# One hand-set line for the gates, the first conv tiles and w_out's sums: a hybrid attention and mLSTM encoder layer on one core

## The chip, the core and the metric

The kernel runs on one core of one Trainium2 chip. The metric is the device time of one execution in microseconds (us); the number given for a kernel is the median over its runs. All data and results are f32. Engines carry the short names of the profile: PE multiplies matrices (PEld is its loading of weights), DVE, ACT and POOL work on vectors, and SP does nothing here but issue DMAs, in the order in which they stand on it. What SP issues for a value that isn't ready yet makes all later DMAs wait.

## The reference, cut to what matters

```python
hmix = rms_norm(x, g_norm1) * (1.0 + scale1) + shift1
q_a, k_a, v_a, q_m, k_m, v_m, o_m, gates = jnp.split(hmix @ w_in, IN_SPLITS, axis=-1)
att = rms_norm(banded_attention(q_a, k_a, v_a, sink), g_attn_out)
qk = silu(centred_dwconv(concat([q_m, k_m]), conv_w, conv_b))        # width 3
i_f, f_f, i_b, f_b = jnp.split(gates + b_gates, 4, axis=-1)
h_m = rms_norm(mlstm(q_m, k_m, v_m, i_f, f_f) + flip(mlstm(flip(...), i_b, f_b)), g_mlstm_out)
h_m = sigmoid(o_m) * h_m
x = x + gate1 * (jnp.concatenate([att, h_m], axis=-1) @ w_out)
gte, up = jnp.split((rms_norm(x, g_norm2) * (1.0 + scale2) + shift2) @ w_ffn_in, 2, axis=-1)
return rms_norm(x + gate2 * ((silu(gte) * up) @ w_ffn_out), g_final)
```

There are 2048 positions of 1024 features, 8 attention heads of 64 and 4 mLSTM heads of 128, and a feed-forward width of 2816. The mLSTM gates pass through a log-sigmoid and running sums and maxima over chunks of 128 positions before any mLSTM product can use them.

## The kernel before

**Stages.** First come norm 1 and the projections with positions on the partitions (v, gates), then the projections with features on the partitions, the four mLSTM heads, the attention, the output projection in eight pairs of 128-position blocks (p0 to p7), norm 2, and the feed-forward network. The two large products, `out_proj` and the network, are formed by Strassen-like schemes with seven products in place of eight: `w_out` is loaded, multiplied by the gate and added up into seven operands, which go to DRAM as `wo_d` (`w_out_ops`); the mixed rows are added up into seven operands by `Pair.s1`, `s4`, `both`, `sums`.

**The fill queue.** PE's instructions stand in an order written out by hand. `fill` holds generators of work that waits for little; `pull(n)` issues the next `n` matmuls of it between the steps of the stage that runs. The projections are such work: `conv_tile(j, h)` makes one 128-feature tile of q or k of head `h` in four blocks of 24 matmuls (`proj_mm` into the PSUM tile `gps`). After each block ACT copies it to `cacc` and its ends to `edge`; DVE adds the two neighbours (L444, L445, and L447, L448 for the seams to the previous block), and `finish` applies silu to the block before (ACT `ctanh`, DVE L435) and stores it to `qk_d`. The order on the other engines is set by a scheduler.

**Gates chain.** After the projections of norm 1 a chain of small steps turns the 16 gate columns (`gn`) into the scan results: PE transposes, ACT and DVE steps on 128x128 tiles (named `gates` in listings), four DVE scans, then the chunk ends go to DRAM and come back as one row (`st_d`, then `sr`), eight short DVE scans over it (`mn`), and the results go out and back again (`rw_d`, then `gates` and `dec`); at the end rows go to `bc_d` and three tiles are transposed (`gates_end`). Beside it PE runs 165 matmuls of `fill`, then the end of the two conv tiles of head 0 and 60 more, and then `mlstm(0)` begins.

**mLSTM heads.** Each head loads `mqk` (q and k) and `mv`, does a backward pass (`kn`, `ktp`, `kvp`: keys times values, state `cb`) and then a forward pass with scores (`sps`, times a decay `sc`) and products (`num`, `den`). POOL prepares `ng` (L592) and `qs` (L597) for the scores. At half of the fill steps of heads 0 and 1, one step of `w_out_ops` is put beside: per unit of 128 columns of each half two products on POOL (L832, 128x256), four differences (L836, 128x128), and stores from `bx`, `by`, `ts`; 16 units in all. `proj_cols` loads each tile's weights and splits them (`whi` on ACT, `wlo` on POOL L234).

**First pair and out_proj.** `Pair` holds the mixed rows of a pair: `square` (L938) forms the squares and their sums `msq` on ACT and POOL, `columns` turns them by a matmul with ones into `aps` on PE, `rsqrt` (L101 to L108) and `diagonal` follow on DVE, PE spreads it as `arb`, `scale` multiplies. For the first pair `first_pair` does this during the attention; `both` (L982) makes two operands `mA`, `mS`. `start_wo(u)` and `finish_wo(u)` load operand `u` of w_out and split it (ACT L911, DVE L912). Inside pair p, step i of the loop sets when the next pair's squares, columns and rsqrt come, and `Rows.step(i)` does norm 2's sums of the pair before: its blocks `n` are turned, added (POOL L1200) and stored to `hop_d` (`put`, L1163). `oslots` and `mring` are rings of free tiles.

Of the kernel before, what the change touches and what calls it, by code (L numbers as in the profile page):

```python
# [36 lines left out]
def hybrid_layer_kernel(  # L37
# [184 lines left out]
    def load_w(src, shape, gate=None):  # L222

        pl, i = wslots[0]
        wslots.rotate(-1)
        r = pl.tile([P, D], F32, tag="wraw", name="wraw", bufs=1)
        hi = pl.tile([P, D], F32R, tag=f"w{i}h", name="whi", bufs=1)
        lo = pl.tile([P, D], F32R, tag=f"w{i}l", name="wlo", bufs=1)
        v = lambda t: t.rearrange("p (a b) -> p a b", a=shape[0])
        sp.dma_start(v(r), src)  # L230
        if gate is not None:
            pool.tensor_tensor(v(r), v(r), gate, MUL)
        act.activation(hi, r, AF.Copy)
        pool.tensor_tensor(lo, r, hi.bitcast(F32), SUB)  # L234
        return v(hi), v(lo)

    def proj_cols(c0):
        return load_w(w_in[:, c0:c0 + P].rearrange("(k p) c -> p k c", p=P), (KT, P))
# [5 lines left out]
    with tc.tile_pool(name="sw", bufs=2, side="right", reuse_waits="tile") as sw:  # L244
# [114 lines left out]
        gn = cp.tile([P, 2, 2, HM, NT], F32, tag="gn", name="gn", bufs=1)  # L359
# [64 lines left out]
    def conv_tile(j, h, w=None):  # L424

        w = w or proj_cols((C_QM, C_KM)[j] + h * P)
# [5 lines left out]
        def finish(a, n):  # L432
            t = s2.tile([P, 512], F32, tag="ctanh", name="ctanh")
            act.activation(t, a, AF.Tanh)  # L434
            dve.scalar_tensor_tensor(a, t, 1.0, a, ADD, MUL)  # L435
            sp.dma_start(qk_d[j, h, n], a)

        for n in range(NB):
            ps = bank("g", "gps")
            yield from proj_mm(ps, w, n)  # L440
# [5 lines left out]
            if prev is not None:  # L446
                dve.scalar_tensor_tensor(a[:, 0:1], edge[:, 2 * n - 1:2 * n], w0, a[:, 0:1], MUL, ADD)  # L447
                dve.scalar_tensor_tensor(prev[:, 511:512], edge[:, 2 * n:2 * n + 1], w2, prev[:, 511:512], MUL, ADD)  # L448
                finish(prev, n - 1)
            prev = a  # L450
        finish(prev, NB - 1)
# [279 lines left out]
    ps = bank("c", "gps")  # L731
    gnf = gn.rearrange("p y d h c -> p y (d h c)")
    for y in range(2):
        pe.transpose(ps[:, y * P:(y + 1) * P], gnf[:, y, :], ident)

    t2 = s2.tile([P, 512], F32, tag="cacc", name="gt2", bufs=3)[:, :P]
    dve.memset(s2.tile([P, 512], F32, tag="ctanh", name="gt3")[:, 0:1], 0.0)
# [7 lines left out]
    ig, fg = gt("ig"), gt("fg")  # L745
    act.activation(ig, ps[:, :P], AF.Copy)
    act.activation(fg, ps[:, P:2 * P], AF.Copy)
    e, u, l = gt("ge"), gt("gu"), gt("gl")
    dve.scalar_tensor_tensor(e, fg, -1.0, fg, MUL, MIN)
    act.activation(e, e, AF.Exp)  # L750
    dve.tensor_scalar(u, e, 1.0, None, ADD)
    act.activation(l, u, AF.Ln)
    dve.scalar_tensor_tensor(t2, u, -1.0, e, ADD, SUB)
    dve.reciprocal(u, u)
    dve.tensor_tensor(t2, t2, u, MUL)
    dve.tensor_tensor(l, t2, l, SUB)
    dve.scalar_tensor_tensor(l, fg, 0.0, l, MIN, ADD)
    b, cm, zr = gt("gb"), gt("gcm"), gt("gz")
    r = cp.tile([P, 2, P], F32, tag="gn", name="grr", bufs=1)[:, 0, :]
    dve.memset(zr, 0.0)  # L760
    lo_, hi_ = slice(0, 64), slice(64, 128)
    dve.tensor_tensor_scan(b[lo_], ones[lo_], l[lo_], 0.0, MUL, ADD)
    dve.tensor_tensor_scan(b[hi_, ::-1], ones[hi_, ::-1], l[hi_, ::-1], 0.0, MUL, ADD)
    dve.tensor_tensor(r, ig, b, SUB)
    dve.tensor_tensor_scan(cm[lo_], zr[lo_], r[lo_], -3e38, ADD, MAX)
    dve.tensor_tensor_scan(cm[hi_, ::-1], zr[hi_, ::-1], r[hi_, ::-1], -3e38, ADD, MAX)
    st = gt("gst", 2)
    for sl, j in ((lo_, 127), (hi_, 0)):
        dve.tensor_copy(st[sl, 0:1], b[sl, j:j + 1])
        dve.tensor_tensor(st[sl, 1:2], b[sl, j:j + 1], cm[sl, j:j + 1], ADD)  # L770
    sp.dma_start(st_d.rearrange("j r -> r j"), st)
    sr = s2.tile([1, 2, P], F32, name="sr", bufs=1)
    sp.dma_start(sr, st_d.rearrange("(o j) r -> o j r", o=1))
    mn = s2.tile([1, P], F32, name="mn", bufs=1)
    rw = s2.tile([1, 3, P], F32, name="rw", bufs=1)
    dve.memset(rw, 0.0)
    for d in range(2):
        for h in range(HM):
            q = slice(d * 64 + h * NT, d * 64 + (h + 1) * NT)
            o_, b_, a_ = mn[:, q], sr[:, 0, q], sr[:, 1, q]  # L780
            if d:
                o_, b_, a_ = o_[:, ::-1], b_[:, ::-1], a_[:, ::-1]
            dve.tensor_tensor_scan(o_, b_, a_, 0.0, ADD, MAX)
    mpv = rw[:, 0, :].rearrange("o (q c) -> o q c", c=NT)
    mnv = mn.rearrange("o (q c) -> o q c", c=NT)
    dve.tensor_copy(mpv[:, 0:4, 1:], mnv[:, 0:4, :-1])
    dve.tensor_copy(mpv[:, 4:8, :-1], mnv[:, 4:8, 1:])
    dve.tensor_tensor(rw[:, 1, :], sr[:, 0, :], mn, SUB)
    dve.tensor_tensor(rw[:, 2, :], rw[:, 1, :], rw[:, 0, :], ADD)
    act.activation(rw[:, 2, :], rw[:, 2, :], AF.Exp)  # L790
    sp.dma_start(rw_d.rearrange("(o j) r -> o j r", o=1), rw)
    mc = gt("gmc", 2)
    sp.dma_start(mc, rw_d[0:2].rearrange("j r -> r j"))
    sp.dma_start(dec, rw_d[2].partition_broadcast(P))
    ux, it, em, wr = gt("gux"), gt("git"), gt("gem"), gt("gwr")
    dve.tensor_scalar(ux, cm, mc[:, 0:1], None, MAX)
    act.activation(it, ux, AF.Exp, bias=mc[:, 0:1], scale=-1.0)
    dve.tensor_scalar(it, it, float(128 ** -0.5), None, MUL)
    dve.tensor_tensor(em, b, ux, ADD)
    act.activation(em, em, AF.Exp, scale=-1.0)  # L800
    act.activation(wr, r, AF.Exp, bias=mc[:, 1:2])
    dve.tensor_scalar(ux, ux, -1.0, None, MUL)
    for d, sl in ((0, lo_), (1, hi_)):
        sp.dma_start(bc_d[:, :, d, :].rearrange("h c t -> (h c) t"), ux[sl])
        sp.dma_start(bc_d[:, :, 2 + d, :].rearrange("h c t -> (h c) t"), it[sl])
    def gates_end():
# [299 lines left out]
    for u in (2, 3):  # L1106
        start_wo(u)
# [657 lines left out]
```

## Time and profile before

| | |
|---|---|
| runs before (us) | 2411.76, 2414.21, 2411.64; median 2411.76 |
| profiled execution | 2408.62 us, span 2406.8 us |
| granted PE clock, mean | 0.976 |
| busy share of the span | PE 95%, PEld 79%, DVE 66%, ACT 44%, POOL 43% |
| DMA | 393.47 MB, mean 163 GB/s |

The profile is one execution. From its span's start, norm 1 and the first projections take until 194 us, the gates chain with the first conv tiles until 258.1, the heads end at 367.2, 475.4, 564.4 and 654.5, the attention at 867, and the first pair of `out_proj` begins at 898. The network runs to the end. Lines (L420 and so on) are those of the kernel before; in listings of the changed kernel the numbers are its own.

### The profile page before, as it was taken

How to read it: one execution, taken by the hardware profiler on the slowest of the kernel's cores; microseconds unless marked ns; L12 is line 12 of the kernel's file. 1: busy time of each engine (PE TensorE's matmuls, PEld its weight loads, DVE VectorE, ACT ScalarE, POOL GpSimd, SP SyncE). 2: the span in 40 equal slices, each digit the busy share in tenths (PEclk: the TensorE clock that was granted, in tenths of full speed). 3: DMA queues.
4: the chain of work that ended last, by engine and by line, in shares of the span. 5: the costliest groups of instructions: out<-in, count | busy, mean ns of one | idle time of the engine just before them, and what ended most of it. 6: DMA issues, size and time to landing. Idle time of an engine off the chain costs nothing.

```text
span 2406.8 us, 32761 instructions
## 1 busy us (share of the span) xinstructions
PE 2275.5 (95%) x10801; PEld 1889.9 (79%) x10801; DVE 1587.8 (66%) x3078; ACT 1062.4 (44%) x2157; POOL 1032.1 (43%) x922
## 2 busy tenths in 40 slices
PE   5998888899899998998999999999999999999998
PEld 4987777788788877777887878788888888888886
DVE  6775575775688858768655776755565536684584
ACT  4523444454377755526444444534433323223352
POOL 1001564343333424434655565555656536493020
PEclk9999999999999999999999999999999999999999
DMA  7574666577675565665343452533333264452452
GB/s 290 175 243 110 180 187 185 151 207 218 172 200 175 172 216 188 228 227 189 123 158 101 153 175 92 210 97 114 101 106 109 88 212 151 136 174 96 135 201 94
DMA packets 370881, 393.47 MB, mean 163 GB/s; under 512 B 24862, under 2 KB 268568, under 8 KB 370712
## 3 DMA queue, kind: packets, MB, share of 16 engines
q1 hardware_dynamic: 370712, 391.39, 51.4%
q8 instruction: 85, 1.39, 0.2%
q14 instruction: 84, 0.69, 0.1%
HBM read 272.12 MB, written 119.19 MB: 163 GB/s over the span
## 4 chain that ended last, share of the span: by engine, by line
PE 72%; DVE 8%; DMA 8%; issue 4%; POOL 3%; ACT 3%; SPq 1%; POOLq 0%; ACTq 0%; DVEq 0%
PE fp L56 11%; PE fp L57 11%; PE fp L58 11%; PE gps L420 8%; PE fo L58 6%; PE fo L56 6%; PE fo L57 5%; PE ops L56 2%; PE ops L57 2%; PE ops L58 2%; DMA bc<-bc_d 1%; PE atp L709 1%; DMA vst_d<-vs 1%; DVE macc L336 1%; PE as L686 1%
## 5 line engine op out<-in xcount | busy, mean ns | idle before, releaser
L420 PE MATMUL gps<-hT,whi 128*128 128x512 f32 x1088 | 403.3, 426 | 4.6 <-ACT ctanh L434 4.6
L56 PE MATMUL fo<-w,ah 128*128 128x512 f32 x616 | 242.3, 393 | 2.5 <-ACT ah L1549 2.5
L58 PE MATMUL fo<-w,al 128*128 128x512 f32 x616 | 242.5, 394 | 0.3 <-DVE al L1550 0.3
L57 PE MATMUL fo<-w,ah 128*128 128x512 f32 x616 | 242.0, 393 | 0.0
L420 PE MATMUL gps<-hT,wlo 128*128 128x512 f32 x544 | 231.6, 426 | 0.0
L420 PEld LDWEIGHTS gps<-hT,whi 128*128 128x128 f32 x1088 | 205.8, 195 | 30.8 <-ACT ctanh L434 5.0
L56 PE MATMUL fp<-T,S 128*128 128x512 f32 x528 | 211.5, 401 | 13.1 <-ACT u L1460 6.7
L57 PE MATMUL fp<-T,S 128*128 128x512 f32 x528 | 209.7, 397 | 0.0
L58 PE MATMUL fp<-T,S 128*128 128x512 f32 x528 | 209.7, 397 | 0.0
L1550 DVE TENSOR_TENSOR al<-al,ah 128x1024 fp32r<-128x1024 f32 x77 | 114.4, 1490 | 126.2 <-ACT ah L1549 126.1
L1307 DVE TENSOR_TENSOR A<-graw,A 128x512 fp32r<-128x512 f32 x86 | 106.2, 1254 | 116.5 <-ACT A L1306 116.5
L1549 ACT ACTIVATE ah<-al 128x1024 fp32r<-128x1024 f32 x77 | 81.5, 1060 | 193.9 <-DMA al<-a_d 191.0
L56 PEld LDWEIGHTS fo<-w,ah 128*128 128x128 f32 x616 | 115.9, 188 | 29.2 <-ACT ah L1549 3.0
L58 PE MATMUL fp<-B,A 128*128 128x512 f32 x352 | 137.6, 391 | 0.0
L56 PE MATMUL fp<-B,A 128*128 128x512 f32 x352 | 137.6, 391 | 0.0
L57 PE MATMUL fp<-B,A 128*128 128x512 f32 x352 | 137.6, 391 | 0.0
L58 PEld LDWEIGHTS fo<-w,al 128*128 128x128 f32 x616 | 115.7, 188 | 27.8 <-DVE al L1550 1.5
L57 PEld LDWEIGHTS fo<-w,ah 128*128 128x128 f32 x616 | 115.9, 188 | 26.4
L56 PEld LDWEIGHTS fp<-T,S 128*128 128x128 f32 x528 | 101.1, 191 | 37.3 <-ACT u L1460 8.2
L702 POOL TENSOR_SCALAR ap<-ap,adn 128x384 f32<-128x384 f32 (+1 forms) x128 | 72.9, 588 | 130.9 <-DVE adn L700 57.2
L1307 DVE TENSOR_TENSOR S<-sf,S 128x512 fp32r<-128x512 f32 x86 | 88.9, 1036 | 47.3 <-ACT S L1306 47.2
L58 PEld LDWEIGHTS fp<-T,S 128*128 128x128 f32 x528 | 101.0, 191 | 22.8
(411 smaller groups left out, 6125.0 us busy)
## 6 DMA issues: line engine op xcount, KB each, us to landing
al<-a_d SPq DMA_DIRECT2D x77, 512.0 KB
wmod<-in_w_mod_dram SPq DMA_DIRECT2D x48, 512.0 KB
graw<-in_w_ffn_in_dram SPq DMA_DIRECT2D x43, 512.0 KB
a_d<-ka SPq DMA_DIRECT2D x66, 256.0 KB
bc<-bc_d SPq DMA_DIRECT2D x64, 256.0 KB
hop_d<-n SPq DMA_DIRECT2D x56, 256.0 KB
a_d<-u SPq DMA_DIRECT2D x55, 256.0 KB
mqk<-qk_d SPq DMA_DIRECT2D x48, 256.0 KB
```

The source lines that it names most:

```text
L56: pe.matmul(o, lh, rh, start=first, stop=False, skip_group_check=skip)
L57: pe.matmul(o, lh, rl, start=False, stop=False, skip_group_check=skip)
L58: pe.matmul(o, ll, rh, start=False, stop=last, skip_group_check=skip)
L336: dve.scalar_tensor_tensor(acc, w[:, i, :], sc_col[:, k + i:k + i + 1], acc, MUL, ADD)
L420: pe.matmul(ps, w[i == 2][:, k, :], hT[n](i == 1, k), start=(k == 0 and i == 0), stop=(k == KT - 1 and i == 2))
L686: pe.matmul(s[:, :NK], self.q[:, g, :], self.kk[:, 0, :NK], start=True, stop=False)
L702: pool.tensor_scalar(self.p[g][:, :self.NK], self.p[g][:, :self.NK], dn[:, g:g + 1], 0.0, MUL, ADD)
L709: pe.transpose(tp[:, g * P:(g + 1) * P], self.p[g][:, i * P:(i + 1) * P], ident)
L1307: dve.tensor_tensor(t[:, 1, :], f, t[:, 0, :].bitcast(F32), SUB)
L1549: act.activation(ah, al.bitcast(F32), AF.Copy)
L1550: dve.tensor_tensor(al, al.bitcast(F32), ah.bitcast(F32), SUB)
```

## The change

It rewrites the order around the gates chain and moves w_out's sums into it.

- `gates()` and `w_out_ops()` become generators that yield the number of the next matmul of `fill` at which to go on. A loop over 252 matmuls (two conv tiles and 60 more) steps both by these numbers, and in it DVE, ACT, POOL and SP keep the order of the code as PE does already.
- w_out's units are twice as wide: 8 units instead of 16, each with two products of 128x512 and four differences of 128x256, all in that stretch; the heads have none. Tiles for them are taken from the rings of tiles that the heads use later (`mqk` with 4, `bc` with 3, `og`, `hst`).
- In the first two conv tiles `finish` of a block is put at matmuls 6 and 14 of the next block. The weights of the third tile are loaded at matmul 100 and split at 130, the last block of head 0 (`load_last`) comes at 192, and the chain's final transposes at 140.
- `first_pair` keeps only loads, squares and their sums, beside the attention; its columns, rsqrt, diagonal, scale and `sums` come between the attention and p0, where six of the seven `both` (before: four) and `finish_wo` 1 to 4 (before: 1 to 3) now stand too. In p0 there remain `finish_wo` at steps 5 and 12 (before: 0, 6 and 12) and `both` at step 8 (before: 2, 5 and 8).
- In all pairs `columns` moves from step 7 to 9, rsqrt from 8 to 10, the previous pair's scale from 12 to 13, and the sums of norm 2 by about one step; loads of the second kind come at 8 instead of 10. The second T3 of a pair is put in the tile `oth`, no longer in the ring of nine tiles from which `new` takes.
- Three rings take the weight tiles `w1` ahead of `w0`.

```diff
-    pull(165)
-    gates_end()
+    steps = [gates(), w_out_ops()]
+    due = [0, next(steps[1])]
     hand.enter_context(tc.manual_schedule(engines={mybir.EngineType.PE}))
+    win.enter_context(tc.manual_schedule(engines={getattr(mybir.EngineType, e) for e in ("DVE", "Activation", "Pool", "SP")}))
...
+    for i in range(2 * 96 + 60):
+        for j, g in enumerate(steps):
+            while due[j] <= i:
+                due[j] = next(g)
+        if i == 100:
+            w3 = cols_steps(C_KM + P)
+            next(w3)
...
+        elif i == 192:
+            last = load_last(0)
+        pull(1)
+    win.close()
...
     for h in range(HM):
-        i = 0
-        while any(f is g for f in fill for g in convs[h]):
-            pull(1)
-            i += 1
-            if i % 2 == 0:
-                next(wops, None)
-        last = load_last(h)
-        for i in range(60):
-            pull(1)
-            if i % 2 == 0:
-                next(wops, None)
+        if h:
+            for g in convs[h]:
+                finish_fill(g)
+            last = load_last(h)
+            pull(60)
         mlstm(h, 3, 8, last)
...
+                bx, by = ready
+                pool.tensor_tensor(bx, bx, gb, MUL)
+                yield at + 6
+                pool.tensor_tensor(by, by, gb, MUL)
+                yield at + 8
+                for o in out_:
+                    sp.dma_start(*o)
+                ta = s2.tile([P, 2, 256], F32, tag="bc", name="ts", bufs=3)
+                tb = s2.tile([P, 2, 256], F32, tag="hst", name="ts")
+                for t, f, g in ((ta[:, 1], bx[:, 1], bx[:, 0]), (tb[:, 0], by[:, 1], bx[:, 1]),
+                                (ta[:, 0], by[:, 1], ta[:, 1]), (tb[:, 1], by[:, 0], ta[:, 0])):
+                    pool.tensor_tensor(t, f, g, SUB)
+                    yield at + 12
+                yield at + 18
+                if (c_, k) != (1, 3):
+                    ready = w_out_load(*((c_, k + 1) if k < 3 else (1, 0)))
...
+                at += 26
...
+        yield 44
+        sp.dma_start(st_d.rearrange("j r -> r j"), st)
...
+        yield 64
...
+            dve.tensor_tensor_scan(o_, b_, a_, 0.0, ADD, MAX)
...
+        yield 81
+        sp.dma_start(rw_d.rearrange("(o j) r -> o j r", o=1), rw)
...
+            for i, _ in enumerate(proj_mm(ps, w, n)):
+                if end and i in (6, 14):
+                    next(end, None)
+                yield True
...
-                if i in (0, 6, 12):
-                    finish_wo(4 + i // 6)
-                if i in (2, 5, 8):
+                if i in (5, 12):
+                    finish_wo(4 + (i + 2) // 7)
+                if i == 8:
                     cur.both()
...
-                if i == 7:
+                if i == 9:
                     ps = bank("a", "aps")
...
+                t3 = wp.tile([P, 512], F32, tag="oth", name="n3", bufs=1) if g else self.new()
```

SP's rows in the gates chain before, from the store of the gate row to the second return of the chain; `mv` is head 0's first load of values:

```order
L411 DMA gate_d<-mod 128x8x1
L407 DMA vaug_d<-va 128x516
L510 DMA mv<-vaug_d 128x4x129 x2
L771 DMA st_d<-gates 128x2x1
L773 DMA sr<-st_d 1x256
L436 DMA qk_d<-cacc 128x512
L791 DMA rw_d<-rw 1x384
L436 DMA qk_d<-cacc 128x512
L793 DMA gates<-rw_d 128x2x1
L794 DMA dec<-rw_d 128x128
```

SP's rows there in the changed kernel; the loads and the six stores of w_out's first unit and the loads of its second stand directly ahead of the first row:

```order
L787 DMA st_d<-gates 128x2x1
L789 DMA sr<-st_d 1x256
L844 DMA bx<-in_w_out_dram 128x2x256
L844 DMA by<-in_w_out_dram 128x2x256
L870 DMA wo_d<-bx 128x256
L870 DMA wo_d<-by 128x256 x2
L870 DMA wo_d<-ts 128x256 x2
L870 DMA wo_d<-ts 128x2x256
L438 DMA qk_d<-cacc 128x512
L844 DMA bx<-in_w_out_dram 128x2x256
L844 DMA by<-in_w_out_dram 128x2x256
L810 DMA rw_d<-rw 1x384
```

The chain's stores now stand between w_out's loads and stores, and `mv` comes only after w_out's seventh unit.

POOL's rows in head 0 before, a little after its first scores are prepared:

```order
L234 TENSOR_TENSOR wlo<-wraw,whi 128x1024
L832 TENSOR_TENSOR bx<-bx,gb 128x256
L836 TENSOR_TENSOR ts<-bx 128x128
L597 TENSOR_TENSOR qs<-mqk,bc 128x256 x2
L832 TENSOR_TENSOR by<-by,gb 128x256
L836 TENSOR_TENSOR ts<-by,bx 128x128
L836 TENSOR_TENSOR ts<-by,ts 128x128 x2
L592 TENSOR_TENSOR ng<-bc,maskb 128x256 x2
L597 TENSOR_TENSOR qs<-mqk,bc 128x256
```

POOL's rows in the changed kernel from w_out's last unit into head 0:

```order
L865 TENSOR_TENSOR bx<-bx,gb 128x512
L867 TENSOR_TENSOR by<-by,gb 128x512
L875 TENSOR_TENSOR ts<-bx 128x256
L875 TENSOR_TENSOR ts<-by,bx 128x256
L875 TENSOR_TENSOR ts<-by,ts 128x256 x2
L233 TENSOR_TENSOR wlo<-wraw,whi 128x1024
L601 TENSOR_TENSOR ng<-bc,maskb 128x256
L606 TENSOR_TENSOR qs<-mqk,bc 128x256
L601 TENSOR_TENSOR ng<-bc,maskb 128x256
L606 TENSOR_TENSOR qs<-mqk,bc 128x256
```

No work of w_out stands among `ng` and `qs` any more; all of it stands ahead of the first `ng`.

DVE's rows before at the beginning of p0 (L958 and L955 scale the second pair, `xr` takes a finished product of p0):

```order
L912 TENSOR_TENSOR wo<-wo 128x1024 x4
L958 SCALAR_TENSOR_TENSOR mm<-og,mm 128x1024
L955 SCALAR_TENSOR_TENSOR ma<-ma,cols,arb 128x2x128 x4
L982 TENSOR_TENSOR mS_10626<-ma,mS_10626 128x512
L1090 TENSOR_TENSOR xr<-xr,ops 128x512
L982 TENSOR_TENSOR mS_10644<-mm,mS_10644 128x512
L912 TENSOR_TENSOR wo<-wo 128x1024 x2
```

DVE's rows there in the changed kernel:

```order
L968 TENSOR_TENSOR wo<-wo 128x1024 x2
L1038 TENSOR_TENSOR mS_10472<-ma,mS_10472 128x512
L1038 TENSOR_TENSOR mS_10475<-mm,mS_10475 128x512
L1014 SCALAR_TENSOR_TENSOR mm<-og,mm 128x1024
L1011 SCALAR_TENSOR_TENSOR ma<-ma,cols,arb 128x2x128 x4
L1142 TENSOR_TENSOR xr<-xr,ops 128x512
L968 TENSOR_TENSOR wo<-wo 128x1024 x2
```

Two of the four `wo` rows now stand ahead of the last operands of the first pair, and no operand stands between the scale of the second pair and the first `xr`.

More of the change, by code (lines that the diff above doesn't have):

```diff
@@ L448, in conv_tile @@
                 dve.scalar_tensor_tensor(prev[:, 511:512], edge[:, 2 * n:2 * n + 1], w2, prev[:, 511:512], MUL, ADD)
-                finish(prev, n - 1)
+                end = finish(prev, n - 1)
+                if not ws_:
+                    deque(end, 0)
             prev = a
-        finish(prev, NB - 1)
+        for f in (end, finish(prev, NB - 1)):
+            deque(f, 0)
     def qk_att(pl, tags, j):
@@ L766, in hybrid_layer_kernel @@
[L766 to L785, printed above, removed]
@@ L843, in hybrid_layer_kernel, with w_out_load, w_out_gate @@
-    wops = w_out_ops()
-    hand = ExitStack()
+        yield 1 << 30
+    def w_out_load(c_, k):
+        r = [s2.tile([P, 2, 256], F32, tag="mqk", name=t, bufs=4) for t in ("bx", "by")]
+        for t, k_ in zip(r, (k, k + 4)):
+            sp.dma_start(t, w_out[k_ * P:(k_ + 1) * P].rearrange("p (m c) -> p m c", m=2)[:, :, c_ * 256:(c_ + 1) * 256])
+        return r
+    def w_out_gate(c_):
+        gb = (wp.tile([P, 2, 256], F32, tag="oth", name="gb", bufs=1) if c_ else
+              s2.tile([P, 2, 256], F32, tag="og", name="gb", bufs=1))
+        for m in range(2):
+            sp.dma_start(gb[:, m, :], gate_d[0, m * 512 + c_ * 256:m * 512 + (c_ + 1) * 256].partition_broadcast(P))
+        return gb
@@ L873, in hybrid_layer_kernel @@
         finish_fill(g)
-    assert not fill and not later and next(wops, None) is None
-    wqs.close()
+    assert not fill and not later
     s2s.close()
@@ L1104, in hybrid_layer_kernel @@
     xr = [load_xr(nxt.tt)]
+    ps = bank("a", "aps")
+    for i in range(2):
+        pe.matmul(ps[:, i:i + 1], nxt.t[:, 2 + i], ones[:, 0:1], start=True, stop=True)
+    nxt.diagonal(rsqrt(w0, ps[:, :2], 2, 512, "ar", 1), nxt.t[:, 0:2])
     finish_fill(lasts[1])
@@ L1107, in hybrid_layer_kernel @@
         start_wo(u)
+    pull(10)
+    nxt.scale()
+    finish_wo(1)
+    nxt.sums(nxt.t.rearrange("p k t -> p (k t)"))
     nxt.both()
@@ L1116, in hybrid_layer_kernel @@
         nx2.square(i, sq[:, i])
-    pull(16)
+    finish_wo(2)
+    finish_fill(lasts[2])
+    for u in (4, 5):
+        start_wo(u)
     ps = bank("a", "aps")
@@ L1134, in hybrid_layer_kernel @@
     start_wo(6)
+    for _ in range(2):
+        nxt.both()
     OPS = ("B11", "B21", "T2", "T1", "T3", "B22", "T4")
```

257 lines of the change are left out of this document (139 added, 118 removed).

## The prediction, made blind

> **What bounds the kernel.** I read the page's first and fourth parts, then a table of stages, then the list of waits stage by stage.
>
> ```profile
> span 2406.8 us, 32761 instructions
> ...
> PE 2275.5 (95%) x10801; PEld 1889.9 (79%) x10801; DVE 1587.8 (66%) x3078; ACT 1062.4 (44%) x2157; POOL 1032.1 (43%) x922
> ...
> PE 72%; DVE 8%; DMA 8%; issue 4%; POOL 3%; ACT 3%; SPq 1%; POOLq 0%; ACTq 0%; DVEq 0%
> ```
>
> PE is busy 95% of the span and carries 72% of the chain that ended last. So the time that can be won without taking matmuls away is PE's idle time, and the extra length of matmuls after idle time. The table of stages says where both lie. Its columns are the stretch, its length, busy us (and instructions) of PE, PEld, DVE, ACT and POOL, PE's granted clock, DMA share and GB/s.
>
> ```profile
> 194.00:258.10 64.10, 59.54 (x260) 48.79 (x258) 33.00 (x79) 22.77 (x49) 14.86 (x19) 0.97 0.44 119
> 258.10:367.20 109.10, 90.65 (x475) 76.11 (x474) 69.66 (x233) 46.18 (x144) 62.20 (x93) 0.91 0.65 186
> 367.20:475.40 108.20, 90.85 (x482) 75.76 (x481) 72.01 (x234) 46.68 (x146) 49.39 (x67) 0.92 0.58 171
> 475.40:564.40 89.00, 85.61 (x488) 72.94 (x486) 59.48 (x213) 42.22 (x132) 32.05 (x38) 0.98 0.71 203
> 654.50:867.00 212.50, 205.29 (x1137) 175.00 (x1138) 171.73 (x500) 161.50 (x431) 84.86 (x137) 1.00 0.63 186
> 867.00:900.00 33.00, 31.48 (x140) 25.73 (x139) 13.35 (x25) 11.27 (x17) 7.09 (x6) 0.97 0.79 257
> 900.00:930.00 30.00, 22.47 (x84) 17.50 (x83) 27.62 (x44) 15.39 (x24) 9.72 (x8) 0.83 0.40 128
> ```
>
> Rows two to four are mLSTM heads 0, 1 and 2. They issue nearly the same number of matmuls (475, 482, 488), but heads 0 and 1 take 109.1 and 108.2 us and head 2 takes 89.0. POOL is busy 62.2 and 49.4 us in the first two and 32.1 in the third, which has nothing of w_out. The last row, the start of p0, has PE idle for 7.5 of 30 us and DVE busy for 27.6.
>
> **Part 1: the heads lose w_out.** PE's waits in heads 0 and 1, and then in head 2 (engine, line waited at, who ended the wait, us in total, times, longest):
>
> ```profile
> PE sps L599 <- DVE sc L601: 12.1, 6, 3.7
> PE ktp L538 <- ACT og L648: 5.1, 1, 5.1
> PE kvp L548 <- DVE den L629: 5.0, 1, 5.0
> PE sps L599 <- DMA mqk<-qk_d: 4.8, 1, 4.8
> ```
>
> ```profile
> PE kvp L548 <- DVE den L629: 1.8, 1, 1.8
> PE sps L599 <- DVE sc L601: 0.9, 1, 0.9
> ```
>
> POOL's and SP's own waits between 150 and 600 us say what made these late:
>
> ```profile
> POOL bx L832 <- DMA bx<-in_w_out_dram: 47.7, 13, 11.3
> ```
>
> ```profile
> SPq L529 <- POOL qs L597: 47.3, 28, 4.6
> SPq L839 <- POOL bx L832: 30.4, 12, 4.1
> ```
>
> POOL stood 47.7 us before w_out's `bx`, and `ng`, which the scores need, is queued behind it in the order listings. SP stood 30.4 us before stores of `bx`, and `mqk`, `mv` and `bc` loads are queued behind these. Without w_out both queues hold only the head's own work, as in head 2. If heads 0 and 1 came down to head 2's time, that would be 20.1 + 19.2 = 39.3 us. But they keep something that head 2 has less of: conv tiles, whose sums and silu run on DVE. DVE is busy 69.7 and 72.0 us there against 59.5, 23 us more for both heads; I put a third of it, 8 us, on the path, since the scores wait for DVE in head 2 as well. That makes 39 less 8: **-31 us**, from -24 (half of the waits that look like w_out's remain somewhere) to -38. No cover is needed for this: the POOL work of w_out is moved ahead, and its DMAs as well.
>
> **Part 2: the gates window gains w_out.** What the chain's returns cost now, from SP's rows (start, length, line), DVE's first scan over the returned row, and PE:
>
> ```profile
> 204.63 1.32 SPq L510 DMA_DIRECT2D mv<-vaug_d  x2
> 206.05 0.45 SPq L771 DMA_DIRECT2D st_d<-gates  x1
> 214.17 0.25 SPq L773 DMA_DIRECT2D sr<-st_d  x1
> ```
>
> ```profile
> 216.95 0.78 DVE L783 TENSOR_TENSOR_SCAN mn<-sr 1x16 f32<-1x16 f32 x8 [7.31 <-DMA sr<-st_d]
> ```
>
> ```profile
> 220.57 1.19 PE L420 MATMUL gps<-hT,whi 128*128 128x512 f32 x2 [4.56 <-ACT ctanh L434]
> ```
>
> The chain's store goes out at 206.05, SP stands for it until 214.17, the row is back at 216.95, and only then does DVE get to the third conv block, so PE waits 4.56 us for a free `gps`. The stretch has no other wait of that size. In the changed order the third block's sums still stand behind those scans, so the wait stays and moves with the chain. What makes the chain later: the first block's two sums now come ahead of the chain's second half; `st_d` stands behind six stores of w_out's first unit, and `rw_d` behind the second unit's stores and the fourth unit's loads. The stores also share DMA queues with the gate and value stores, which were landed by 204.63, when `mv` could go. That gives `st_d` at about 209 to 214, 3 to 8 us later.
>
> POOL's own price is worked out from the same operations at other sizes (mean ns behind the bar):
>
> ```profile
> L597 POOL TENSOR_TENSOR qs<-mqk,bc 128x256 f32<-128x256 f32 x64 | 47.6, 746 | 27.2 <-DMA mqk<-qk_d 16.6 <-PE num L622 6.8 <-issue 2.7
> ...
> L639 POOL TENSOR_TENSOR hst<-hst,mry 128x512 f32<-128x512 f32 x16 | 16.6, 1040 | 36.3 <-DVE mry L108 26.7 <-ACT mjk L636 3.7 <-DVE den L629 2.7
> ```
>
> ```profile
> 261.96 0.56 SPq L828 DMA_DIRECT2D bx<-in_w_out_dram  x1
> ```
>
> ```profile
> 265.26 0.90 POOL L832 TENSOR_TENSOR bx<-bx,gb 128x256 f32<-128x256 f32 x1 [4.79 <-DMA bx<-in_w_out_dram]
> ```
>
> A unit is two products of 128x512 (1.04 us, or 1.5 if doubled from 128x256) and four differences of 128x256: 2 x 1.04 + 4 x 0.746 = 5.1 us, with the other price 6.0. Eight units are 41 to 48 us of a window of 64, and a load takes 265.26 - 261.96 = 3.3 us. Loads of a unit need the tiles of the unit two before, so its stores must have landed. While SP stands at `sr`, until about 219, POOL can have only the first two units; six are left, and at 7 to 8 us each (5.1 to 6.0, and what is not hidden of store and load) they end at 261 to 267, when the window, delayed itself, ends at 262 to 266. Their last stores stand on SP ahead of most of head 0's `mqk` and `mv`, so head 0 may begin a few us late. I add up: the chain 3 to 8 us later, matmuls at a lower clock behind a longer wait (1 to 2), and 0 to 6 us for the loads of head 0: **+10 us**, the upper middle of 4 to 16. The low end is -6, if the wait of 4.56 us and its slow matmuls go, since `finish` is now set between the matmuls of the next block. The high end is +20, the rival below.
>
> The final transposes now stand at matmul 140. A matmul takes 59.54 / 260 = 0.229 us, so PE is there at 194 + 32 = 226 plus its wait, at 232 to 238, and the chain's second return and its exponentials must be through by then, within some 12 us of the scans. If they are late by a few us, PE waits that long; this is inside the 4 to 16. The third tile's weights at matmuls 100 and 130 are an existing load and split at another place: 0, hidden by the first two tiles' matmuls.
>
> **Part 3: the first pair.** Waits of PE inside the attention, then from 867 to 930, and then of p4 and p5 (1000 to 1040):
>
> ```profile
> PE aps L989 <- DVE aptl L127: 1.7, 2, 1.0
> ...
> PE arb L953 <- DVE aptl L127: 1.3, 1, 1.3
> ```
>
> ```profile
> PE aps L989 <- POOL msq L942: 4.9, 4, 2.7
> PE ops L56 <- DVE xr L1090: 4.2, 2, 3.5
> ```
>
> ```profile
> PE aps L989 <- POOL msq L942: 5.9, 4, 2.2
> ```
>
> ```profile
> 997.83 1.29 POOL L1200 TENSOR_TENSOR n<-n,n 128x512 f32<-128x512 f32 x1 [3.03 <-DMA hop_d<-n]
> ```
>
> In the attention the columns and the spread of the first pair's norm wait behind attention work on DVE, 3.0 us; those instructions are moved behind it: **-3.0**, from -3 to 0. What remains there, squares and POOL sums, lies beside PE's 205 of 212 us.
>
> At p0's start PE idles 7.5 us, most of it for `msq` and for `xr`. DVE's order puts four `wo` rows and the scale of the second pair ahead of the first `xr`; in the changed order two `wo` rows, two operands and the scale of the second pair. What is taken out of p0 lands in the stretch before (867 to 900), where DVE is busy 13.4 of 33 us and so has 20 us of room, and PE has the last tiles of the fill queue to do. The first pair's own new chain (columns, rsqrt of 12 small DVE steps, spread, scale) is covered by the 10 matmuls and by start_wo, which may not last. The squares' waits move from step 7 to 9, two steps later, of three matmuls each: 6 x 0.229 = 1.4 us, by which such waits get shorter. Of 7.5 us of idling and about 3 us of slower matmuls (clock 0.83) I take **-6**, from -10 to -2.
>
> In p4 and p5 the waits for `msq` stem from `n`: POOL waited 3.03 us for a store to land because the ring of nine was full. The second T3 in `oth` takes one use of the ring away, and columns stand later: **-5** of 5.9 and of the slow matmuls behind them, from -9 to -3. The remaining pairs show no such wait, so the shift by a step costs nothing there.
>
> Ring orders (`w1` ahead of `w0`): 0, from -1 to 1. The feed-forward network is the same code.
>
> **The sum.** -31 + 10 - 3 - 6 - 5 = -35 us against the profiled execution of 2408.6, thus 2373.6. The median of the runs shown is 3.1 us above it, so I forecast **2377 us**.
>
> **Rivals.** *B, POOL and DVE block each other in the window.* The row of a one-column DVE step with two operands in SBUF (ns least, median, most), and two conv steps in head 0, where POOL is busy 57% of the time:
>
> ```profile
> L448 DVE SCALAR_TENSOR_TENSOR cacc<-edge,cvw,cacc x24: 208/212/1743, 206.7 to 496.5; 128x1 f32<-128x1 f32 x24
> ```
>
> ```profile
> L435 DVE SCALAR_TENSOR_TENSOR cacc<-ctanh,cacc 128x512 f32<-128x512 f32 x10 | 7.8, 776 | 1.8 <-ACT ctanh L434 1.6
> L445 DVE SCALAR_TENSOR_TENSOR cacc<-gps,cvw,cacc 128x511 f32<-128x511 f32 x10 | 7.4, 740 | 0.0
> ```
>
> A step of 0.21 us sometimes takes 1.74: it is held for up to 1.5 us. L445, which reads one operand from PSUM, isn't lengthened. In the window POOL would be busy most of the time with steps of 0.75 to 1.0 us, and the chain has about 20 steps of two SBUF operands. At half a POOL step each (0.5) that is 10 us more on the chain, and three such steps in each of the window's ten conv blocks are 15 us more on DVE, which is busy 33.0 of the 64.1 us and can still take them. Then part 2 is +20 to +25 and the time 2387 to 2392; I take 2390. The Trainium skill, page "SBUF — State Buffer", section "Who interferes with whom", states that a DVE instruction with two SBUF inputs contends with a GpSimd instruction that reads SBUF, and that the loser fully blocks. By that rule, the trace agrees: 1743 ns against 212, and 740 for the step with a PSUM operand. It speaks against putting the sums beside the chain.
>
> *C, the window is smooth:* `st_d` is as early as now, the 4.56 us go, and POOL ends in time. -31 - 5 - 3 - 6 - 5 = -50, and 2362. Against it stand SP's six stores ahead of `st_d`.
>
> *D, the heads stay slow:* PE's waits for DVE `sc` (12.1 us) would be due to DVE at 65%, and conv work, not to POOL. Then part 1 gives -8 and the time is 2400. Against it: POOL's 47.7 us of waiting before `bx`, with `ng` behind.
>
> *E, the other side:* the units are paced by their round trip through SP's one line, load 3.3, POOL 5 to 6, store 3 to 5, since a load stands behind stores that wait for POOL, and head 0's loads stand behind the last unit. The gains without part 2 are 45 us; head 0 would have to begin at 258 + 45 = 303. With two units done by 219 and some 4 us of loads at the end, that is (303 - 219 - 4) / 6 = 13.3 us per unit: from there on the kernel is slower, at 14.5 us per unit by 7 us: 2419. For it speaks that SP stood 30.4 us before stores of `bx`; against it that two units have tiles at a time.
>
> **How the numbers follow.** Chances: the forecast 0.45, B 0.2, C 0.15, D 0.1, E 0.1. The likeliest case gives 2377 with its own range of 2366 to 2386. The range of 2356 to 2402 takes in C, B and D and leaves out E, and what is worse than their ends. A measurement of this kernel can tell about 0.2% (4.8 us) from no change. The forecast, B, C and most of D are faster: 0.86; same (2407 to 2416.6), an end of D and the threshold of E: 0.05; slower: 0.09.
>
> **What the changed profile would show.** Right: heads 0 and 1 at 90 to 95 us each with no POOL wait for `bx` in them; the window ending at 262 to 270, one PE wait of 5 to 12 us for `ctanh` in it, `st_d` at 209 to 214; no `aps` or `arb` wait in the attention; p0's start with less than 4 us of PE idling. Wrong: `sps` waits of over 8 us for DVE in heads 0 and 1 with POOL free (D); a first `ktp` of head 0 that waits over 10 us for `mqk` (E, or B if DVE's small steps in the window take over 0.7 us each); new `aps` waits at 880 to 900, where the first pair's chain has little cover, which would eat part 3.

## The result, and the profile after

The changed kernel took 2396.32 us (median of 9 runs, 2391.49 to 2403.93) against 2411.64 us (9 runs): ratio 0.9941, interval 0.9924 to 0.9957. That is 15.3 us less, where 35 were forecast. Its profiled execution took 2403.93 us, the longest of the nine, so single stages of it are read together with those of the experiments that share their code.

First come rows of the view of one tile of PE, of the kernel before and then of the changed one. Behind the count stand ns (least, median, most) and the time of the first and the last; the first times cut the span into stages.

```profile
L538 PE MATMUL ktp<-ident,mqk x64: 270/272/476, 258.1 to 580.9; 128*128 128x128 f32 x64
L686 PE MATMUL as<-ak,aq x128: 276/333/420, 654.7 to 856.9; 128*128 128x384 f32 x112, 128*128 128x256 f32 x16
L56 PE MATMUL ops<-wo,mS x128: 387/393/792, 909.5 to 1086.0; 128*128 128x512 f32 x128
L56 PE MATMUL fp<-T,S x528: 389/389/795, 1094.8 to 1962.3; 128*128 128x512 f32 x176
```

```profile
L547 PE MATMUL ktp<-ident,mqk x64: 270/271/329, 277.5 to 570.7; 128*128 128x128 f32 x64
L695 PE MATMUL as<-ak,aq x128: 276/335/550, 645.7 to 847.9; 128*128 128x384 f32 x112, 128*128 128x256 f32 x16
L56 PE MATMUL ops<-wo,mS x128: 387/393/792, 899.5 to 1078.8; 128*128 128x512 f32 x128
L56 PE MATMUL fp<-T,S x528: 389/389/794, 1087.7 to 1954.5; 128*128 128x512 f32 x176
```

| stage | before | after | forecast change | change |
|---|---|---|---|---|
| window: last store of values (194.6, 196.5) to head 0's `ktp` | 63.5 | 81.0 | +10 | +17.5 |
| heads: to the first `as` | 396.6 | 368.2 | -31 | -28.4 |
| attention and p0's beginning: to the first `ops` | 254.8 | 253.8 | -9 | -1.0 |
| `out_proj`: to the first `fp` | 185.3 | 188.2 | -5 | +2.9 |
| network: to the end of the span | 1312.0 | 1314.4 | 0 | +2.4 |

The heads in the table of stages (the second and third row are heads 0 and 1, without POOL's waits for `bx`), ahead of them the window:

```profile
194.00:277.50 83.50, 63.63 (x268) 51.36 (x266) 38.34 (x75) 19.04 (x40) 48.37 (x49) 0.89 0.64 185
277.50:371.10 93.60, 84.21 (x473) 70.97 (x472) 69.34 (x236) 48.87 (x151) 36.38 (x41) 0.98 0.60 181
371.10:464.10 93.00, 84.56 (x482) 70.30 (x481) 70.81 (x234) 47.15 (x147) 34.58 (x39) 1.00 0.53 159
```

Heads 0 and 1 fell from 109.1 and 108.2 us to 93.6 and 93.0, and DVE is as busy in them as before. The window holds POOL's 48 us, and PE idles 20 of its 83 us there. Where PE's wait comes from is read backwards through four engines: PE, DVE, SP, POOL (the number in brackets is the idle time before the row):

```profile
232.91 1.19 PE L420 MATMUL gps<-hT,whi 128*128 128x512 f32 x2 [14.99 <-DVE cacc L451]
```

```profile
228.85 0.78 DVE L800 TENSOR_TENSOR_SCAN mn<-sr 1x16 f32<-1x16 f32 x8 [13.16 <-DMA sr<-st_d]
```

```profile
213.67 2.56 SPq L870 DMA_DIRECT2D wo_d<-ts  x3
216.33 0.41 SPq L787 DMA_DIRECT2D st_d<-gates  x1
226.21 0.25 SPq L789 DMA_DIRECT2D sr<-st_d  x1
```

```profile
209.71 1.29 POOL L865 TENSOR_TENSOR bx<-bx,gb 128x512 f32<-128x512 f32 x1 [22.39 <-DMA gb<-gate_d]
```

PE waits 15 us for a free `gps`, since the third conv block's sums stand on DVE behind the scans over `sr`. `st_d` went out only at 216.33, behind the first unit's stores, though its data were ready at 208.8. Those stores waited for POOL, whose first product waited until 209.71 for `gb`. PE's waits at p0's start, and then in the other pairs:

```profile
PE ops L56 <- DVE xr L1142: 5.2, 1, 5.2
PE aps L1045 <- POOL msq L998: 5.0, 2, 4.3
```

```profile
PE ops L56 <- DVE xr L1142: 9.1, 7, 2.5
```

The waits for `msq` in p4 and p5 are gone, and seven waits for `xr` stand in their place. At p0's start PE waits 5.0 us for `msq` and 5.2 for `xr`, no less than before (4.9 and 4.2). PE's rows for `xr` there, two of the kernel before and one of the changed:

```profile
909.54 0.79 PE L56 MATMUL ops<-wo,mS 128*128 128x512 f32 x1 [0.66 <-DVE xr L1090]
920.45 0.77 PE L56 MATMUL ops<-wo,mS 128*128 128x512 f32 x1 [3.52 <-DVE xr L1090]
```

```profile
910.94 0.79 PE L56 MATMUL ops<-wo,mS 128*128 128x512 f32 x1 [5.20 <-DVE xr L1142]
```

DVE's rows ahead of the longest of the seven other waits, and PE's row there:

```profile
999.97 0.15 DVE L101 TENSOR_SCALAR ar2v<-aps 128x2 f32<-128x2 f32 x1
...
1005.26 0.48 DVE L1004 TENSOR_SCALAR dg<-ident,ar2y 128x128 f32<-128x128 f32 x2
1005.65 0.68 DVE L1142 TENSOR_TENSOR xr<-xr,ops 128x512 f32<-128x512 f32 x1
```

```profile
1006.39 0.50 PE L56 MATMUL ops<-wo,mS 128*128 128x512 f32 x1 [2.48 <-DVE xr L1142]
```

The next pair's rsqrt and diagonal hold DVE from 999.97 to 1005.65, and `xr`, which frees PE's bank, stands directly behind them.

### The profile page after: what moved, and what is told of

Read it like the earlier page. It is cut to its first block, busy times and chain, and to the rows that moved or that the text cites. A ratio compares the mean times of both kernels' runs of the same rounds, so it can differ in the third digit from the quotient of the medians.

```text
span 2402.1 us, 32619 instructions
## 1 busy us (share of the span) xinstructions
PE 2265.9 (94%) x10801; PEld 1877.0 (78%) x10801; DVE 1595.0 (66%) x3075; ACT 1063.0 (44%) x2159; POOL 1028.5 (43%) x876
## 4 chain that ended last, share of the span: by engine, by line
PE 49%; DVE 4%; DMA 2%; issue 1%; ACT 1%; SPq 0%; POOL 0%; DVEq 0%; ACTq 0%; POOLq 0%
PE fp L56 11%; PE fp L57 11%; PE fp L58 11%; PE fo L58 5%; PE fo L56 5%; PE fo L57 5%; DMA al<-a_d 1%; PE ops L56 1%; PE ops L58 1%; PE ops L57 1%; DVE S L1369 1%; DVE ra L1737 0%; DVE w L1618 0%; DVE A L1369 0%; DMA x1r<-x_d 0%
## 5 line engine op out<-in xcount | busy, mean ns | idle before, releaser
L420 PEld LDWEIGHTS gps<-hT,whi 128*128 128x128 f32 x1088 | 204.1, 193 | 45.9 <-issue 21.4
L56 PEld LDWEIGHTS fp<-T,S 128*128 128x128 f32 x528 | 100.7, 191 | 39.0 <-ACT u L1522 10.1
L58 PEld LDWEIGHTS fp<-T,S 128*128 128x128 f32 x528 | 100.4, 190 | 22.5
L57 PEld LDWEIGHTS fp<-T,S 128*128 128x128 f32 x528 | 100.6, 191 | 21.6
```

What stands on the lines that cost most here:

```text
L56: pe.matmul(o, lh, rh, start=first, stop=False, skip_group_check=skip)
L57: pe.matmul(o, lh, rl, start=False, stop=False, skip_group_check=skip)
L58: pe.matmul(o, ll, rh, start=False, stop=last, skip_group_check=skip)
L420: pe.matmul(ps, w[i == 2][:, k, :], hT[n](i == 1, k), start=(k == 0 and i == 0), stop=(k == KT - 1 and i == 2))
```

## The experiments

**The two halves of the change.** `win_only` is the kernel before with the new window (gates, conv tiles, w_out); `tail_only` is the kernel before with the rest. The ratios below are to the kernel before as it ran beside each experiment, with medians of 2410.5 to 2414.1 us.

> The kernel before with the gates window, the conv tiles and w_out's sums of the change, and nothing of its out_proj part. Theory W (the window gives back most of what the heads win, the out_proj part is worth about nothing): first ktp of head 0 at 277 instead of 258, heads 0 and 1 at 93 us each, so 19 - 31 = -12 us: 2400. Rival T (the out_proj part is worth its forecast 14 us, and the profile of the changed kernel was a slow one): the window part alone is worth about 1 us, 2411.

> The kernel before with the first pair, p0, norm 2's steps and the ring orders of the change, and the gates window of before. Theory W: the waits for msq in p4 and p5 (5.9 us) go, waits for xr (9 us) come in their place in seven pairs, p0 keeps a wait of 5 us: between -3 and +3 us, 2409 to 2415. Rival T: -14 us, 2398.

Measured: `win_only` 2390.44 us, ratio 0.9927 (0.9912 to 0.9941); `tail_only` 2411.37 us, 1.0006 (0.9988 to 1.0023). The tail is worth nothing, as theory W had it; its `out_proj` stretch is 188.4 us. The window alone wins more than W's 12 us: its profile has the window at 78.4 us and the heads at 365.2 (31.4 less than before). Over the six profiles with this order (the changed kernel, `win_only`, and `gate2_late`, `rsqrt_back`, `rsqrt_t3_back`, `no_first` below) the window is 76.5 to 81.0 us, 78.8 on average. That is 15 us longer than the 63.5 of before and 12 longer than the 66.6 of `tail_only`, which has before's window. The profile of the changed kernel showed the longest one.

**The chain's store ahead of w_out's.**

```diff
-        yield 44
+        yield 33
         sp.dma_start(st_d.rearrange("j r -> r j"), st)
+        yield 44
```

> The changed kernel with one edit: the store st_d is issued ahead of the six stores of w_out's first unit (yield 33 instead of 44), the load sr behind them as it was. Theory Q (st_d is late because it stands on SP behind stores that wait for POOL): st_d goes out at about 209.5 instead of 216.3, PE's wait of 15.0 us falls to about 8, and the time falls by 7 us against the changed kernel, to 2389. Rival L (the chain is late because DMAs of w_out share the way and the landing sets it): st_d goes out early but sr still lands at 228, the wait stays at 14 to 15, 2396. Rival P (POOL and DVE block each other): no change either, since the chain's steps are as long as before.

Measured: 2389.59 us, 0.9924 (0.9905 to 0.9943), 6.7 us less than the changed kernel.

```profile
207.15 0.38 SPq L787 DMA_DIRECT2D st_d<-gates  x1
...
216.05 0.24 SPq L790 DMA_DIRECT2D sr<-st_d  x1
```

```profile
223.14 1.19 PE L420 MATMUL gps<-hT,whi 128*128 128x512 f32 x2 [6.91 <-DVE cacc L451]
```

The store goes out at 207.15, PE's wait falls from 15.0 to 6.9 us, and the window is 72.1 us: theory Q's place and size.

**Why `gb` is late.** `gb_now` loads the gate row from an input (`b_mod` in place of `gate_d`), `gate2_late` puts the second gate store behind the window in the code, and `gate2_win` into the window:

```diff
-        sp.dma_start(gate_d[1].rearrange("(k p) -> p k", p=P), mod[:, 5, :])
...
+        elif i == 240:
+            sp.dma_start(gate_d[1].rearrange("(k p) -> p k", p=P), mod[:, 5, :])
```

> The changed kernel with w_out's gate row loaded from the bias input instead of from gate_d, so that its load waits for no store (the gate is left out of the result but for its bias). Theory Q: POOL's first unit starts at about 202 instead of 209.7, its stores go out by 209, st_d at about 210, PE's wait falls to 8 or 9 us, and w_out's last unit ends some us earlier: 6 to 9 us faster than the changed kernel, 2388 to 2390. Rival P: POOL's first two units now lie on the chain's DVE steps (204 to 209), which grow from 4.8 to 9 us or more; the wait stays over 12 us, and the gain is under 3 us.

> The changed kernel with one edit: the second store of a gate row, 1024 single elements from 128x8x1, goes out after the window instead of directly ahead of the last value store and w_out's first loads. Theory G (the gate row for w_out lands at 208 to 210, from whatever source, because it stands in the DMA queues behind this store of single elements): SP's 5 us stop at the fourth load goes, w_out's first product starts at about 201 instead of 209.7, st_d goes out at about 210 instead of 216, PE's wait falls from 15 to about 8 us, 6 us faster than the changed kernel's profile. Rival (the row's broadcast to 128 partitions itself takes 10 us): the first product stays at 208 to 210 and so does all that follows.

> The changed kernel with the second store of a gate row really late: it stands in the window's own order on SP, at matmul 240. (In gate2_late the scheduler still put it at 192.5.) Theory G (the store of 1024 single elements holds up what stands behind it in the DMA queues): w_out's first loads land by 200, SP does not stop at the fourth load, w_out's first product starts at about 200 instead of 209.7, st_d goes out at 209 to 210, PE's wait is 8 us, the profile 7 us below the changed kernel's. Rival (the landing of these loads has another cause): first product at 208 or later, PE's wait 12 to 16 us.

Measured: `gb_now` 2396.19 us, first product at 208.44: the source of the row doesn't matter, so Q's reading of `gb` fell. `gate2_late` says nothing, since the scheduler still issued the store at 192.55 (2395.78 us). In `gate2_win` the first product starts at 200.38:

```profile
200.38 1.29 POOL L864 TENSOR_TENSOR bx<-bx,gb 128x512 f32<-128x512 f32 x1 [14.90 <-DMA gb<-gate_d]
```

Theory G holds: the store of 1024 single elements had held up all that stood behind it. But the time did not fall (2399.28 us, 0.9950, 0.9933 to 0.9967): the window is 74.4 us, 4 shorter than in the six profiles, and the heads take 373.0, 8 longer than in `win_only`. Two things worked against it. The chain's scans on DVE, of `gate2_win` and then of `combo` below, where POOL's first product comes at 205.87, after them:

```profile
205.51 0.81 DVE L777 TENSOR_TENSOR_SCAN gates<-ones_r,gates 64x128 f32<-64x128 f32 x1
206.36 1.20 DVE L778 TENSOR_TENSOR gates<-gates 128x128 f32<-128x128 f32 x1
207.59 1.39 DVE L779 TENSOR_TENSOR_SCAN gates<-gates 64x128 f32<-64x128 f32 x1
```

```profile
202.00 0.42 DVE L777 TENSOR_TENSOR_SCAN gates<-ones_r,gates 64x128 f32<-64x128 f32 x1
202.45 0.29 DVE L778 TENSOR_TENSOR gates<-gates 128x128 f32<-128x128 f32 x1
202.78 0.42 DVE L779 TENSOR_TENSOR_SCAN gates<-gates 64x128 f32<-64x128 f32 x1
```

With POOL beside them the steps take two to four times as long; the chain from L767 to L784 takes 200.62 to 211.0, 10.4 us, instead of 199.28 to 204.1, 4.8 us. This is rival B's mechanism. It agrees with the rule that stands beside that rival, from the Trainium skill, page "SBUF — State Buffer", section "Who interferes with whom". And the store, put ahead of head 0's loads, holds up these:

```profile
281.84 0.48 PE L546 MATMUL ktp<-ident,mqk 128*128 128x128 f32 x1 [10.42 <-DMA mqk<-qk_d]
```

**Without POOL's work, and without w_out in the chain.** `no_sums` drops POOL's products and differences; `late_w` starts the units at matmul 112, one per 16:

```diff
-                pool.tensor_tensor(bx, bx, gb, MUL)
...
-                pool.tensor_tensor(by, by, gb, MUL)
...
```

```diff
+        yield 112
         ready = w_out_load(0, 0)
...
-                at += 26
+                at += 16
```

> The changed kernel without w_out's products and differences on POOL; the stores write what was loaded (of w_out's operands the sums and the gate are left out), so SP's order and all DMAs stay. Theory Q (the window is late since SP waits for POOL's units and the chain stands behind): st_d at about 209, PE's first wait 7 us, the units no longer set when head 0 may load, first product of head 0 at 261 to 264, 8 to 12 us faster than the changed kernel. Rival E' (the DMAs' round trip through one line is the bound, POOL or not): first product at 270 or later, gain under 4 us. Heads 0 and 1 stay at 93 us each in both.

> The changed kernel with w_out's units moved behind the chain: the first at matmul 112, then one every 16 matmuls, so that no DMA of w_out stands among the chain's returns. If the window's 14 to 19 us come from the chain behind w_out's DMAs: PE's first wait 5 to 8 us, then no wait over 3 us, but w_out's eight units end 15 us later than in the changed kernel, and head 0's mqk is waited for: first product of head 0 at 268 to 274. If it is the DMA round trip of the units: from 222 eight units at 6 to 7 us each end at 272 to 278, first product at 275 to 282 and no gain, 2396 or more.

Measured: `no_sums` 2397.65 us, 0.9943 (0.9927 to 0.9960), head 0 at 275.9: Q's 8 to 12 us did not come, E' holds. `st_d` goes out at 209.03 and PE's first wait is 9.67 us, but the window is as long without any sum (82.2 us). SP's rows of one unit there, from its loads to the next:

```profile
225.16 0.55 SPq L844 DMA_DIRECT2D bx<-in_w_out_dram  x1
225.84 0.55 SPq L844 DMA_DIRECT2D by<-in_w_out_dram  x1
...
229.79 0.43 SPq L868 DMA_DIRECT2D wo_d<-bx  x1
230.26 0.93 SPq L868 DMA_DIRECT2D wo_d<-by  x2
...
235.28 0.55 SPq L844 DMA_DIRECT2D bx<-in_w_out_dram  x1
```

The next load of `bx` stands at 235.28, and the fourth after the first at 261.78: 9.2 us per unit without POOL's work, and 8.4 in the changed kernel (231.49 to 265.24). So POOL's work does not pace the units; SP's line does. In the unit shown, 5.6 of 10.1 us are SP's own issuing (w_out's DMAs, the chain's and a conv store), and two waits of 2.0 us each come before the chain's return `gates` and before the next load. How much of the window each kind of DMA costs was not taken apart. `late_w` frees the chain (one wait of 6.3 us) and gives it all back: 2411.65 us, 0.9987 (0.9972 to 1.0003).

```profile
PE ktp L547 <- DMA mqk<-qk_d: 23.3, 1, 23.3
```

Head 0's first `ktp` came at 271.0, as the first expectation had it, but the next load of `mqk` stands behind the last units, and neither expectation had a price for that.

**rsqrt back, T3 back, first pair back.** `rsqrt_back` is the changed kernel with

```diff
-                if i == 9:
+                if i == 7:
                     ps = bank("a", "aps")
...
-                if i == 10:
+                if i == 8:
```

`rsqrt_t3_back` also puts the second T3 back into the ring (`t3 = self.new()`), and `no_first` is `rsqrt_back` with the first pair and p0 of the kernel before.

> The changed kernel with the next pair's columns at step 7 and its rsqrt at step 8 again (as in the kernel before); the second T3 stays in its own tile, the sums of norm 2 stay a step later. Theory X (moved to step 10, rsqrt's dozen small DVE steps stand ahead of the xr that frees PE's bank): the seven waits for xr between 930 and 1088, 9.1 us, fall under 2, no wait for msq comes back since the ring has its tile, and out_proj from its first product to the network's first takes 179 to 182 us instead of 188. Rival (the shift is needed for msq): the waits of p4 and p5 for msq, 5.9 us, come back, and the stretch takes 185 us as before.

> As rsqrt_back, and the second T3 in the ring of nine tiles again. Theory X with the ring as the cause of the waits in p4 and p5: 5 to 6 us of waits for msq there, the stretch 185 us, as in the kernel before. Rival (it was norm 2's one step that ended them): no such waits, 179 to 182.

> As rsqrt_back, but with first_pair, the stretch ahead of p0 and p0's own steps of the kernel before: only the window, the ring orders, T3's tile and the one step of norm 2 remain of the change. If moving the first pair's products is worth nothing: 2381 to 2386, as rsqrt_back (2382.8). If it is worth the forecast 9 us: 2390 to 2394. If it costs (a wait of 4.3 us for msq and one of 4.7 us for xr stand there now, 4.9 and 4.2 before): 2378 to 2381.

Measured: `rsqrt_back` 2382.83 us, 0.9876 (0.9855 to 0.9897); the stretch of `out_proj` 179.4 us instead of 188.2. `rsqrt_t3_back` 2392.85 us, 0.9914 (0.9892 to 0.9936); 184.7 us. `no_first` 2383.34 us, 0.9884 (0.9870 to 0.9899); 180.0 us. The waits after p0's start, of `rsqrt_back` and of `rsqrt_t3_back`:

```profile
PE ops L56 <- DVE xr L1142: 2.8, 2, 1.5
PE aps L1045 <- POOL msq L998: 1.3, 2, 0.7
```

```profile
PE aps L1045 <- POOL msq L998: 6.0, 4, 2.3
```

Theory X holds in both: rsqrt at step 10 stood ahead of `xr`, and the ring of nine had caused the waits for `msq`. The waits for `xr` fell from 9.1 to 2.8 us, not quite under the 2 that was expected. T3's own tile is worth 184.7 - 179.4 = 5.3 us, the moved rsqrt with its columns costs 188.2 - 179.4 = 8.8; the stretch is 187.9 to 188.4 us in all eight profiles with rsqrt at step 10. The median of `rsqrt_back` fell by 13.5 us against the changed kernel; the stretch explains 8.8, and no run shows where the rest comes from. The first pair's move, as it was made, is worth nothing: 252.6 us from `as` to `ops` in both `rsqrt_back` and `no_first`.

**Better versions.** `combo` has st_first's and rsqrt_back's edits, the scans at matmul 76 (`yield 64` to `yield 76`) and gate2_late's, which again left the store where it was. `best2` adds gate2_win's store and puts `nx2.square` ahead of `nxt.sums`; `best3` is `combo` with the squares alone; `best4` is `best3` with late_w's units. The squares' edit:

```diff
+    sq = w1.tile([P, 2, 4, P], F32, tag="msq", name="msq", bufs=1)
+    for i in range(2):
+        nx2.square(i, sq[:, i])
     nxt.sums(nxt.t.rearrange("p k t -> p (k t)"))
...
-    sq = w1.tile([P, 2, 4, P], F32, tag="msq", name="msq", bufs=1)
-    for i in range(2):
-        nx2.square(i, sq[:, i])
     finish_wo(2)
```

> The changed kernel with four edits: the second gate store after the window, st_d ahead of the first unit's stores, the scans over the returned row at matmul 76 so that the third conv block's sums come ahead of them, rsqrt at step 8. If the three causes are right: no PE wait over 3 us in the window, head 0's first product at 258 to 262, heads as in the changed kernel, out_proj 8 us shorter: 2372 to 2378. If w_out's units and head 0's loads behind them bound the window instead: first product at 267 or later, and 2382 to 2388.

> combo with the second gate store at matmul 240, and with the second pair's squares put ahead of the first pair's sums on POOL, so that msq is there when PE wants aps. If both theories hold: the wait of 4.3 us for msq at 878 goes, st_d goes out at 204 or earlier with w_out's first unit 5 us earlier, and the time is 2364 to 2370, against 2373.8 of combo. If the sums behind the squares make the first operands late instead: a wait of about 3 us for mA or mS in their place, and 2370 to 2375.

> combo with the second pair's squares ahead of the first pair's sums on POOL, and nothing else (the second gate store stays where it is, where it keeps POOL's first unit behind the chain's DVE steps). The wait of 4.3 us for msq goes as in best2, the stretch from the attention's first to out_proj's first product takes 245 to 247 us instead of 252, and the time is 2365 to 2369, under combo's 2373.8. Rival: best2's short stretch came from its later start (transfers of wo that were already landed), and the time stays at 2372 to 2375.

> best3 with w_out's units moved behind the chain as in late_w. If the chain behind w_out's DMAs is what is left of the window: first product of head 0 at 262 to 268 instead of 264.7 in combo, 2362 to 2368. If the units bound it: 270 or later and 2372 to 2380, slower than best3.

Measured: `combo` 2373.76 us, 0.9843 (0.9823 to 0.9862); `best2` 2388.80, 0.9898 (0.9884 to 0.9913); `best3` 2370.08, 0.9819 (0.9790 to 0.9848); `best4` 2394.17, 0.9916 (0.9887 to 0.9944). `combo` kept a wait of 6.9 us in the window, now because ACT's fourth block waits (3.6 us) for a tile whose store `qk_d` stands on SP behind w_out; the scans' edit won nothing to be seen (the window is 72.9 us, in `st_first` 72.1). `best2` lost to the gate store and to POOL beside the chain, as `gate2_win` did, but its stretch from `as` to `ops` is 244.9 us. `best3` keeps that (246.6) without the loss. PE's waits from 850 to 930 in `combo` and in `best3`:

```profile
PE aps L1046 <- POOL msq L999: 5.0, 2, 4.3
PE ops L56 <- DVE xr L1143: 4.7, 1, 4.7
```

```profile
PE ops L56 <- DVE xr L1143: 4.7, 1, 4.7
```

So this wait for `msq` came from the change: the first pair's sums stand on POOL ahead of the second pair's squares. The stretch from `as` to `ops` is 5.4 us shorter for it (252.0 in `combo`); the two medians differ by 3.7 us, which their intervals don't separate. `best3` is 44.1 us below the median of before beside it (ratio: 1.8% less), 1.1 us above the range it was expected in, and beats both kernels. In `best4` the units behind the chain bound head 0 again.

## Why the prediction was right in part and wrong in size

The direction was right, the size was not: -35 us was forecast and -15.3 came. That 2396.32 lies within 2356 to 2402 is luck. The forecast's own case ends at 2386, and the stretch above it was there for rivals B and D, and neither of them set this time. About 20 us are missing: 2 to 5 in the window, 8 in the first pair and p0, 8 in `out_proj`.

- **Heads, -31: right.** The eleven profiles with the new window and an undisturbed head 0 give 363.6 to 368.2 us instead of 396.6, and the heads keep the DVE work that I left in.
- **Window, +10: too small; 12 to 15 on average, and 17.5 in the profile of the changed kernel.** The chain of causes stood in the prediction (SP's order, the scans ahead of the third block), but three prices were too low. `st_d` was put 3 to 8 us later; counted from the last store of values it went out 8 to 10 us later, and the wait behind it grew from 4.6 to 15.0 us. The first unit's load was priced at 3.3 us by a quiet row; its first product began 11 us after the load of `gb` was issued, behind the store of single elements. And the units were put at 7 to 8 us each; they took 8.4.
- **Rival B had the mechanism, not the case.** In the changed kernel the gate store happens to keep POOL back until the chain's first half is through. Where POOL came earlier, the chain took 5.6 us longer, about half of B's 10.
- **Rival E had the bound.** SP's line sets the units' pace, with POOL's work or without (`no_sums`), at 8.4 us each, far under the 13.3 from which it would have made the kernel slower.
- **First pair and p0, -9: wrong, nothing was won.** The step that failed is "What is taken out of p0 lands in the stretch before (867 to 900), where DVE is busy 13.4 of 33 us and so has 20 us of room": the room was counted on DVE and not on POOL. There the first pair's sums now stand ahead of the second pair's squares, which made a wait of 5.0 us for `msq` at 878 (1.5 before). The prediction named "new `aps` waits at 880 to 900" only as a sign and gave them no price. The third pair's waits for `msq` at p0's start (3.4 us) did go, but not by the move from step 7 to 9: in `combo`, with step 7 again, they stayed away. And the reading of `xr` was wrong. It blamed the four `wo` rows and the scale ahead of the first `xr`. But the wait at that first `xr` was 0.66 us. The longer one, 3.52, comes at 920, behind the next pair's rsqrt, which the change leaves ahead of `xr`; it grew to 5.20.
- **p4 and p5, -5: right for T3 (5.3 us), wrong in "the shift by a step costs nothing there".** In the other pairs rsqrt at step 10 stands directly ahead of an `xr` for which PE waits; that cost 8.8 us. The profile of before showed no wait there, and this only said that the old place was free.

With 12 to 15 us for the window the terms make -17 to -14 (-31 for the heads, -1 and +3 for the other two), around the measured -15.3.

## What to carry to other kernels

A step that is moved must be priced at its new place: look up what stands behind it on its engine there, since the old place's lack of waits says nothing on the new one. When work is put beside a chain whose steps each wait for the one before, ask for each engine and queue what the chain's next step stands behind; here one store moved ahead of others on SP won 7 us, and one pair's squares moved ahead of another's sums on POOL made their stretch 5 us shorter. Take the time for a load that lands in a busy queue from a row behind the same neighbours, not from a quiet stretch.

## What was not expected of the hardware

The store of one gate row, 1024 single elements, holds up what is issued behind it wherever it stands. Ahead of `gb`, the first product begins 11 to 13 us after that load's issue (198.29 to 209.71 in the changed kernel), and without the store 5.4 us after it (194.96 to 200.38 in `gate2_win`). Ahead of head 0's `mqk`, PE waits 10.4 us. The changed kernel's row for that time, DMA share and GB/s last:

```profile
198.00:205.00 7.00, 7.00 (x32) 5.79 (x32) 2.42 (x4) 1.90 (x4) 0.00 (x0) 1.00 0.59 14
```

The queues are busy 59% of the time and move 14 GB/s. The chain's own store of 256 elements keeps SP from `sr` for 8 to 10 us in every profile here. In the kernel before (209 to 214) and in the changed one (218 to 226) the profile shows no DMA traffic in most of that time; why, no run shows.
